# Sharing three accumulator banks between scores and projections, giving attention outputs two, and running gate tiles in halves

## The chip, the cores and the metric

The kernel runs on one core of a Trainium2 chip. The metric is the device time of one execution in microseconds (us); lower is better. PE is TensorE (matmuls), PEld its weight loads, DVE is VectorE, ACT is ScalarE, POOL is GpSimd, SP is SyncE, whose queue issues most transfers. PSUM is the memory that PE writes its sums into; this kernel uses it as eight banks of 128 x 512 fp32.

## The reference, cut to what matters

Two transformer-like blocks act on 512 tokens of width 1024. The change is in the first one:

```python
h = rmsnorm(x, norm_mix_g)
qkv_a, q_b, k_b, v_b, gate_logits = split(h @ w_in)       # 7424 columns
for gi, (window, dil) in enumerate(((128,1),(512,4),(2048,16))):
    ...   # 8 heads of 64: rmsnorm + rope on q, k; windowed attention; keep o and logsumexp
o_a = sum(softmax(lses) * outs)                          # the three groups combined
o_b = gqa_blocked_attention(q_b, k_b, v_b)               # dense, 8 query heads, 2 key heads
gates = sigmoid(gate_logits + b_gate)                    # 2 x 1024 columns
merged = gates[0] * (o_a @ w_proj_a) + gates[1] * (o_b @ w_proj_b)
x = x + merged @ w_out
...   # then top-4-of-32 experts, then the second block (two layers)
```

## The kernel before

**Order.** Python loops write out every instruction; a planner then orders them at build time, engine by engine. It walks its own estimate of the time, gives earlier-written instructions precedence among those that are ready, and hands a tile of a pool to whichever tile asks when one is free. On the chip each engine runs its list in that fixed order. `tc.issue_after(ins)` adds one rule: what is written under it comes behind `ins` on that engine.

**Precision.** Each fp32 operand is split into a high and a low part (`split`: a copy on ACT, L49, and a subtraction on DVE, L50). `mm3` (L82 to L84) makes three matmuls of each product, `mm2` (L74, L75) two.

**Stages.** `block1` runs three dilated groups (`dilated(g)`) and one `dense` stage as generators, so that the key projections of a stage are written before the last attention step of the stage ahead of it. A stage projects keys, values and queries (`proj_tok`: 24 matmuls into one PSUM tile `M`, which `headnorm` reads with two ACT copies, L277 and L278, or `split` reads for values). Then it takes four blocks of 128 tokens. In group 0 a block is four steps with two score tiles `S` each (`scores`); in groups 1 and 2 it is two steps with one score tile each (L550 to L555); in the dense stage four steps with two score tiles each. A step goes: scores on PE, row maximum on DVE (L211), exponentials on ACT (L216), transposes on PE into `T` (L231), `split` of the transposed probabilities into `Ph`, `Pl`, and `values`: matmuls into one PSUM tile `O`, which two ACT copies (L248, into `of`) or two splits (into `obh`, `obl`; some of these tiles bear the name `kzh`, `kzl`) empty.

**PSUM.** `M` has two banks, `S` two, `F` one, `T` two, `O` one: eight.

**Gate tiles.** `filler(n)` makes n of 16 gate tiles: two loads of 512 x 128 weights, each split on ACT and DVE, 24 matmuls into the `F` bank, a tanh on ACT (L363), and a store on POOL's queue. Its matmuls come behind the last matmul that was written before it. `FILL` says where: four in group 2, one behind each block (L572), and twelve in the dense stage, one in each of its first twelve steps between scores and probabilities (L506).

**Behind the attention.** `bank()` gives tiles of `S` and `M` in turn to the output projections (L605) and to `w_out` (L628, L637); `half` in `route` uses `F` and `S` for the router's logits (L703) and `O` for counts (L732). The expert stage and the second block follow.

Of the kernel before, what the change touches and what calls it, by code (L numbers as in the profile page):

```python
# [9 lines left out]
F32 = mybir.dt.float32  # L10
# [7 lines left out]
PSUM = bass.MemoryType.PSUM  # L18
# [3 lines left out]
S = 512  # L22
NT = 4
KT = 8
# [14 lines left out]
class Kern:  # L39
# [257 lines left out]

    def proj_tok(self, xh, xl, W, i, perm, ncol, ps=None):
        if ps is None:
            ps = self.psM.tile([128, 512], F32, name="M", tag="M")  # L300
        ps = ps[:, :ncol]
        sl = self.tok(i, perm)
        self.mm3(ps, [((xh[:, k, sl], xl[:, k, sl]), W[k]) for k in range(len(W))])
        return ps

    def block1(self):
        nc, tc, a = self.nc, self.tc, self.a
# [1 line left out]
        R = dict(reuse_waits="tile")  # L309
        es, pe, rs_, re = ExitStack(), ExitStack(), ExitStack(), ExitStack()  # L310
        P = lambda n, b, **k: (pe if "space" in k else es).enter_context(tc.tile_pool(name=n, bufs=b, **k))
        self.psM, self.psS, psF = (P(n, b, space=PSUM) for n, b in (("psM", 2), ("psS", 2), ("psF", 1)))
        self.psT, self.psO = P("psT", 2, space=PSUM), P("psO", 1, space=PSUM)
        self.psF = lambda: psF.tile([128, 512], F32, name="F", tag="F")
        c1 = P("c1", 1)
        O = lambda n, b: re.enter_context(tc.tile_pool(name=n, bufs=b, side="right", **R))
# [23 lines left out]
        nc.sync.dma_start(bg, a["b_gate"])  # L340
        nc.vector.tensor_scalar(bg, bg, 0.5, None, op0=ALU.mult)
        xk = [(xh[:, k], xl[:, k]) for k in range(KT)]
        todo = list(range(16))

        FILL = ((0, 0, 0, 0), (0, 0, 0, 0), (1, 1, 1, 1), (1, 1, 1, 1, 1, 1, 1, 1, 1, 1, 1, 1, 0, 0, 0, 0))
        turn = [0]

        def bank():

            turn[0] += 1  # L350
            pool, tag = (self.psS, "S") if turn[0] % 2 else (self.psM, "M")
            return pool.tile([128, 512], F32, name=tag, tag=tag)

        def filler(n=1):

            for n in [todo.pop(0) for _ in range(min(n, len(todo)))]:
                after = self.last_mm.ins
                W = self.weight(a["w_in"][:, 5376 + n * 128:5504 + n * 128], KT, 128, self.fw, 4)
                ps = self.psF()
                with tc.issue_after(after):  # L360
                    self.mm3(ps, [(W[k], xk[k]) for k in range(KT)])
                gt = stg.tile([128, S], F32, name="gl")
                nc.scalar.activation(gt, ps, AF.Tanh, scale=0.5, bias=bg[:, n:n + 1])  # L363
                self.st(GL[n], gt)
# [64 lines left out]

        def scores(q, kh, kl, mk=None):  # L430

            b = self.psS.tile([128, 512], F32, name="S", tag="S")[:, :kh.shape[-1]]
            if mk is not None:
                nc.tensor.matmul(b, lhsT=self.ident_b, rhs=mk, start=True, stop=False)
            self.mm2(b, q, kh, kl, start=mk is None)
            return b[:, None, :]
# [35 lines left out]
        def dense():  # L472
            tb = trig("b", 64)
            kA, kB = self.rope_tables(rp, *tb, a["kn_b"], 64, "kb")
            qA, qB = self.rope_tables(rp, *tb, a["qn_b"], 64, "qb")
            W = self.weight(a["w_in"][:, 5120:5376], KT, 256)
            vs = []
            for i in range(NT):
                ps = self.proj_tok(xh, xl, W, i, False, 256)
                kk = st.tile([128, 2, 2, 64], F32, name="kkb", bufs=1)  # L480
# [11 lines left out]
                if i == 1:  # L492
                    yield
            W = self.weight(a["w_in"][:, 4608:5120], KT, 512)
            q = [queries(self.proj_tok(xh, xl, W, 0, False, 512), qA, qB, 64, 0, True)]
            for i in range(NT):
# [5 lines left out]
                for p in range(4):  # L502
                    v = p // 2
                    ms = self.small.tile([128, 4], F32, name="md", bufs=4)
                    sc = [scores(q[i][:, p, s], kd[0][:, v], kd[1][:, v]) for s in range(2)]
                    filler(FILL[3][4 * i + p])  # L506
                    pr = self.probs(sc, 1, NT, SC, ms[:, :2], ms[:, 2:], True)
# [5 lines left out]
        def dilated(g, tr):  # L513
            perm = g > 0
            kA, kB = self.rope_tables(rp, *tr, a["kn_a"][g], 16, "k")
            qA, qB = self.rope_tables(rp, *tr, a["qn_a"][g], 16, "q")
            W = self.weight(a["w_in"][:, 1536 + 512 * g:2048 + 512 * g], KT, 512)
            for i in range(NT):
                ps = self.proj_tok(xh, xl, W, i, perm, 512)
                kk = st.tile([128, 8, 64], F32, name="kk", tag="qk")  # L520
                self.headnorm(ps, 8, kA, kB, 16, kk, i)
                keys(kk.rearrange("p h e -> p (h e)"), g, i)
                if i == 1:
                    yield
            W = self.weight(a["w_in"][:, 3072 + 512 * g:3584 + 512 * g], KT, 512)
            vs = []
            for i in range(NT):
                ps = self.proj_tok(xh, xl, W, i, perm, 512)
                vh = vp.tile([128, 512], F32R, name="vh")
                vl = vp.tile([128, 512], F32R, name="vl")  # L530
                self.split(vh, vl, ps)
                vs.append((vh, vl))
            W = self.weight(a["w_in"][:, 512 * g:512 + 512 * g], KT, 512)
            q = [queries(self.proj_tok(xh, xl, W, 0, perm, 512), qA, qB, 16, 0, not perm)]
            for i in range(NT):
                if i + 1 < NT:
                    q.append(queries(self.proj_tok(xh, xl, W, i + 1, perm, 512), qA, qB, 16, i + 1, not perm))
                else:
                    yield

                us = st.tile([128, 528], F32, name="us", bufs=3)
                mo_, so_ = us[:, 512:520], us[:, 520:528]
                of = st.tile([128, 4, 128], F32, name="of", bufs=1)
                sl = slice(i * 128, i * 128 + 128)
                pv = lambda j, p: tuple(t[:, p * 128:p * 128 + 128] for t in vs[j])
                if perm:
                    qh, ql = q[i]
                    mk = mask[:, 128:256] if g == 1 else m4
                    for p0 in (0, 2):
                        b = self.psS.tile([128, 2, 2, 128], F32, name="S", tag="S")  # L550
                        nc.tensor.matmul(b, lhsT=self.ident_b, rhs=mk[:, None, None, :].to_broadcast([128, 2, 2, 128]),
                                         start=True, stop=False)
                        for p in (p0, p0 + 1):
                            self.mm3(b[:, p - p0], [((qh[:, p], ql[:, p]), (kz[0][:, p, :, sl], kz[1][:, p, :, sl]))],
                                     start=False, stop=p > p0)  # L555
                        hs = slice(2 * p0, 2 * p0 + 4)
                        pr = self.probs([b.rearrange("p a s k -> p (a s) k")], 4, 1, SC, mo_[:, hs], so_[:, hs])
                        for p in (p0, p0 + 1):
                            self.values([pv(i, p)], pr[p - p0], of[:, p])
                else:  # L560
                    j0, j1 = max(0, i - 1), min(NT, i + 2)
                    mk = mask[:, (j0 - i + 1) * 128:(j1 - i + 1) * 128]
                    for p in range(4):
                        hs = slice(2 * p, 2 * p + 2)
                        ks = slice(j0 * 128, j1 * 128)
                        pr = self.probs([scores(q[i][:, p, s], kz[0][:, p, s, ks], kz[1][:, p, s, ks], mk)
                                         for s in range(2)], 1, j1 - j0, SC, mo_[:, hs], so_[:, hs])
                        self.values([pv(j, p) for j in range(j0, j1)], pr[0], of[:, p])
                ut = transposed(of.rearrange("p a t -> p (a t)"), 4)
                nc.scalar.activation(us[:, :512], ut.rearrange("p a t -> p (a t)"), AF.Copy)  # L570
                self.st(U[g][self.tok(i, perm)], us)
                filler(FILL[g][i])  # L572

        tr = {False: trig("n", 16), True: trig("p", 16)}

# [2 lines left out]
        for n in range(4):  # L578
# [2 lines left out]
                next(stages[n + 1])  # L581
            for _ in stages[n]:
                pass
        filler(16)
        rs_.close()
        at.close()
        mg = O("mg", 1)
# [10 lines left out]
        for br, w, (oh, ol) in ((0, a["w_proj_a"], oa), (1, a["w_proj_b"], ob)):  # L598
            for n in range(KT):
                if n % 4 == 0:  # L600
                    W = self.weight(w[:, n * 128:n * 128 + 512], 4, 512)
# [3 lines left out]
                ps = bank()  # L605
# [21 lines left out]
        for c, W in enumerate(Ws):  # L627
# [7 lines left out]
            for i in range(NT):  # L635
                sl, cs = slice(i * 128, i * 128 + 128), slice(c * 512, c * 512 + 512)
                ps = banks[i] if c == 0 else bank()  # L637
# [11 lines left out]
    def route(self, pool):  # L649

        nc, a, rt = self.nc, self.a, self.rt
# [39 lines left out]
        todo = []  # L691

        def half(i, c, x):
# [6 lines left out]
            xhl[i, c] = [T([128, 4, 128], f"x{s}", F32R, bufs=3) for s in "hl"]  # L700
            self.split(*xhl[i, c], p)
            self.router_act = self.last_act.ins
            ps = self.psF() if i % 2 else self.psS.tile([128, 512], F32, name="S", tag="S")  # L703
            for k in range(4):
                xh, xl = (t[:, k] for t in xhl[i, c])
                nc.tensor.matmul(ps[:, :64], lhsT=xh, rhs=Wr[:, 4 * c + k], start=k == 0, stop=False)
# [826 lines left out]
```

## Time and profile before

| what | value |
|---|---|
| median of 3 runs | 3086.06 us (3082.26 to 3087.57) |
| profiled execution | 3086.88 us, span in the trace 3085.1 us |
| PE busy | 2917.6 us (95% of the span) |
| PEld busy | 2293.6 us (74%) |
| DVE busy | 2250.2 us (73%) |
| ACT busy | 1737.4 us (56%) |
| mean granted TensorE clock | 0.982 |

Busy times are sums over one execution; the profiled execution's own time and its span differ by 1.78 us. The scores of group 0 run from 104 to 187 us, those of group 1 from 195 to 257, of group 2 from 271 to 354, of the dense stage from about 420 to 562; the output projections follow until about 650 us.

### The profile page before, as it was taken

To read this page: it belongs to the slowest core of one execution; us is meant where nothing else is said; L and a number is where in the kernel's file an instruction comes from. 1 tells how busy PE (TensorE), PEld (TensorE's weight loads), DVE (VectorE), ACT (ScalarE), POOL (GpSimd) and SP (SyncE) were. 2 spreads that over 40 slices of the span, in tenths; PEclk is the share of its full clock that TensorE was granted. 3 is DMA by queue.
4 is the path that set the end of the run, shared out by engine and by line. 5 is a ranking of instruction groups with operands and counts; after the bars stand their busy time and mean duration, and the time that the engine had idled before them with its cause. 6 is when DMAs were issued, how large, how long until landed. Compare 5 with 4: busy or idle time off the path is not lost.

```text
span 3085.1 us, 39468 instructions
## 1 busy us (share of the span) xinstructions
PE 2917.6 (95%) x14226; PEld 2293.6 (74%) x14226; DVE 2250.2 (73%) x3789; ACT 1737.4 (56%) x2577; POOL 318.4 (10%) x316
## 2 busy tenths in 40 slices
PE   7999999979999999999999997999999979999998
PEld 6898878766777666666666665878887868888876
DVE  7765577668998999999999997554466585445664
ACT  5555545337777777777777774444454234444532
POOL 0000001001112111111111101011000020110000
PEclk9999999989999999999999999999999989999999
DMA  5122233469999999999999994433536433345262
GB/s 157 63 69 67 76 107 96 129 257 318 366 365 345 354 352 360 355 359 361 356 359 359 349 368 129 133 102 114 113 103 202 148 98 115 112 118 114 89 235 89
DMA packets 405833, 644.92 MB, mean 209 GB/s; under 512 B 23024, under 2 KB 150528, under 8 KB 405632
## 3 DMA queue, kind: packets, MB, share of 16 engines
q1 hardware_dynamic: 385808, 581.67, 56.6%
q0 software_dynamic: 19248, 58.58, 6.4%
q8 instruction: 114, 1.87, 0.3%
q10 hardware_dynamic: 576, 2.10, 0.2%
q14 instruction: 87, 0.71, 0.1%
HBM read 592.10 MB, written 54.36 MB: 210 GB/s over the span
## 4 chain that ended last, share of the span: by engine, by line
PE 74%; DVE 12%; issue 7%; ACT 3%; DMA 3%; SPq 0%; POOL 0%; POOLq 0%; ACTq 0%; DVEq 0%
PE M L82 6%; PE M L83 6%; PE G L82 6%; PE M L84 6%; PE G L84 6%; PE G L83 6%; PE F L82 5%; PE F L83 5%; PE F L84 5%; DVE wlo L50 5%; PE Y L82 4%; PE Y L83 3%; PE Y L84 3%; DMA raw<-in_w_in 1%; PE O L82 1%
## 5 line engine op out<-in xcount | busy, mean ns | idle before, releaser
L50 DVE TENSOR_TENSOR wlo<-raw,whi 128x2048 fp32r<-128x2048 f32 (+4 forms) x642 | 1161.9, 1821 | 274.0 <-ACT whi L49 269.8
L49 ACT ACTIVATE whi<-raw 128x2048 fp32r<-128x2048 f32 (+3 forms) x646 | 972.1, 1532 | 231.3 <-PE M L84 110.3
L82 PE MATMUL G<-wlo,exh 128*96 128x512 f32 x1024 | 410.0, 400 | 4.7 <-ACT exh L49 2.7
L83 PE MATMUL G<-whi,exl 128*96 128x512 f32 x1024 | 404.0, 395 | 1.9 <-DVE exl L50 1.9
L84 PE MATMUL G<-whi,exh 128*96 128x512 f32 x1024 | 403.8, 394 | 0.0
L82 PE MATMUL F<-xl,whi 128*128 128x512 f32 x768 | 311.3, 405 | 17.1 <-DVE fl L1228 10.0
L83 PE MATMUL F<-xh,wlo 128*128 128x512 f32 x768 | 305.3, 398 | 2.3 <-DVE wlo L50 2.3
L84 PE MATMUL F<-xh,whi 128*128 128x512 f32 x768 | 305.6, 398 | 0.0
L82 PE MATMUL M<-wlo,xh 128*128 128x512 f32 (+2 forms) x736 | 278.1, 380 | 12.4 <-POOL wlo L50 3.5
L83 PE MATMUL M<-whi,xl 128*128 128x512 f32 (+2 forms) x736 | 275.2, 374 | 0.0
L84 PE MATMUL M<-whi,xh 128*128 128x512 f32 (+2 forms) x736 | 274.0, 374 | 0.0
L84 PEld LDWEIGHTS G<-whi,exh 128*96 128x96 f32 x1024 | 165.7, 162 | 71.5
L82 PEld LDWEIGHTS G<-wlo,exh 128*96 128x96 f32 x1024 | 165.8, 162 | 70.6 <-ACT exh L49 3.0
L82 PE MATMUL Y<-wlo,ath 128*96 128x512 f32 x512 | 207.4, 405 | 10.6 <-DVE wlo L50 9.9
L83 PEld LDWEIGHTS G<-whi,exl 128*96 128x96 f32 x1024 | 165.7, 162 | 67.3 <-DVE exl L50 2.4
L83 PE MATMUL Y<-whi,atl 128*96 128x512 f32 x512 | 202.4, 395 | 0.1
L84 PE MATMUL Y<-whi,ath 128*96 128x512 f32 x512 | 201.8, 394 | 0.0
L82 PEld LDWEIGHTS M<-wlo,xh 128*128 128x128 f32 x736 | 164.4, 223 | 32.9 <-DVE wlo L50 4.9
L82 PEld LDWEIGHTS F<-xl,whi 128*128 128x128 f32 x768 | 146.0, 190 | 54.9 <-DVE fl L1228 13.5
L83 PEld LDWEIGHTS M<-whi,xl 128*128 128x128 f32 x736 | 165.0, 224 | 13.6
L84 PEld LDWEIGHTS M<-whi,xh 128*128 128x128 f32 x736 | 164.4, 223 | 14.1
L83 PEld LDWEIGHTS F<-xh,wlo 128*128 128x128 f32 x768 | 146.2, 190 | 32.0 <-DVE wlo L50 3.0
(479 smaller groups left out, 5095.3 us busy)
## 6 DMA issues: line engine op xcount, KB each, us to landing
raw<-in_w_gate_up SPq DMA_DIRECT2D x256, 1024.0 KB, 7.0
raw<-in_w_down SPq DMA_DIRECT2D x124, 1024.0 KB, 8.2
raw<-in_w_in SPq DMA_DIRECT2D x154, 512.0 KB, 4.0
GZ<-fl POOLq DMA_DIRECT2D x80, 256.0 KB, 2.4
raw<-in_w_out SPq DMA_DIRECT2D x24, 512.0 KB, 3.9
raw<-in_w_branch SPq DMA_DIRECT2D x24, 512.0 KB, 4.4
gt<-GZ SPq DMA_DIRECT2D x48, 256.0 KB, 3.1
raw<-in_w_in SPq DMA_DIRECT2D x32, 256.0 KB, 3.1
```

The source lines that it names most:

```text
L49: self.last_act = nc.scalar.activation(hi, src, AF.Copy)
L50: self.last_dve = (eng or nc.vector).tensor_sub(lo, src, f(hi))
L82: nc.tensor.matmul(out, lhsT=ah, rhs=bl, start=start and i == 0, stop=False)
L83: nc.tensor.matmul(out, lhsT=al, rhs=bh, start=False, stop=False)
L84: self.last_mm = nc.tensor.matmul(out, lhsT=ah, rhs=bh, start=False, stop=stop and i == n - 1)
```

## The change

The pools `psM` (2) and `psS` (2) become one pool `psM` of three banks; `psO` goes from one bank to two. Gate tiles are made in halves of 12 matmuls: the first half opens the sum in `F`, the second closes it and is followed by tanh and store. The 32 halves are placed between scores and probabilities of a step: none in group 0, one in every second step of group 1 (4), one in every step of group 2 (8), and 2, 1, 1, 1 in the four steps of each dense block (20). `bank()` gives three tiles of `M` and one of `O` in turn, and the router uses `M` in place of `S`.

```diff
-        self.psM, self.psS, psF = (P(n, b, space=PSUM) for n, b in (("psM", 2), ("psS", 2), ("psF", 1)))
-        self.psT, self.psO = P("psT", 2, space=PSUM), P("psO", 1, space=PSUM)
+        self.psM, psF = (P(n, b, space=PSUM) for n, b in (("psM", 3), ("psF", 1)))
+        self.psT, self.psO = P("psT", 2, space=PSUM), P("psO", 2, space=PSUM)
...
-        todo = list(range(16))
-        FILL = ((0, 0, 0, 0), (0, 0, 0, 0), (1, 1, 1, 1), (1, 1, 1, 1, 1, 1, 1, 1, 1, 1, 1, 1, 0, 0, 0, 0))
+        todo = [(n, k0) for n in range(16) for k0 in (0, 4)]
+        FILL = ((0,) * 16, (0, 1) * 4, (1,) * 8, (2, 1, 1, 1) * 4)
...
-            pool, tag = (self.psS, "S") if turn[0] % 2 else (self.psM, "M")
+            pool, tag = (self.psM, "M") if turn[0] % 4 else (self.psO, "O")
...
-            for n in [todo.pop(0) for _ in range(min(n, len(todo)))]:
+            for n, k0 in [todo.pop(0) for _ in range(min(n, len(todo)))]:
                 after = self.last_mm.ins
-                W = self.weight(a["w_in"][:, 5376 + n * 128:5504 + n * 128], KT, 128, self.fw, 4)
-                ps = self.psF()
+                W = self.weight(a["w_in"][k0 * 128:k0 * 128 + 512, 5376 + n * 128:5504 + n * 128], 4, 128, self.fw, 4)
+                if k0 == 0:
+                    self.gbank = self.psF()
+                ps = self.gbank
                 with tc.issue_after(after):
-                    self.mm3(ps, [(W[k], xk[k]) for k in range(KT)])
+                    self.mm3(ps, [(W[k], xk[k0 + k]) for k in range(4)], start=k0 == 0, stop=k0 > 0)
+                if k0 == 0:
+                    continue
...
-            b = self.psS.tile([128, 512], F32, name="S", tag="S")[:, :kh.shape[-1]]
+            b = self.psM.tile([128, 512], F32, name="S", tag="M")[:, :kh.shape[-1]]
...
-                        b = self.psS.tile([128, 2, 2, 128], F32, name="S", tag="S")
+                        b = self.psM.tile([128, 2, 2, 128], F32, name="S", tag="M")
...
+                        filler(FILL[g][2 * i + p0 // 2])
                         hs = slice(2 * p0, 2 * p0 + 4)
...
-                filler(FILL[g][i])
...
-        filler(16)
+        filler(32)
...
-            ps = self.psF() if i % 2 else self.psS.tile([128, 512], F32, name="S", tag="S")
+            ps = self.psF() if i % 2 else self.psM.tile([128, 512], F32, name="S", tag="M")
```

## Rows read from the trace of the kernel before

**Rows 1.** The page: span, and busy time of each engine

```profile
span 3085.1 us, 39468 instructions
PE 2917.6 (95%) x14226; PEld 2293.6 (74%) x14226; DVE 2250.2 (73%) x3789; ACT 1737.4 (56%) x2577; POOL 318.4 (10%) x316
```

**Rows 2.** Busy time by stretch: length, each engine's busy us (instructions), PE clock, DMA

```profile
100.00:190.00 90.00, 80.36 (x460) 73.19 (x460) 63.23 (x190) 51.52 (x141) 9.67 (x19) 1.00 0.12 40
190.00:280.00 90.00, 82.35 (x408) 75.84 (x408) 59.70 (x153) 50.57 (x140) 1.63 (x3) 0.98 0.26 80
280.00:345.00 65.00, 63.39 (x334) 61.10 (x332) 45.95 (x129) 35.34 (x91) 1.08 (x2) 1.00 0.24 74
345.00:420.00 75.00, 67.38 (x353) 56.24 (x352) 40.61 (x135) 38.53 (x107) 4.34 (x8) 0.95 0.27 89
420.00:440.00 20.00, 16.79 (x63) 12.63 (x61) 17.18 (x47) 8.32 (x17) 3.71 (x4) 0.83 0.53 161
440.00:520.00 80.00, 78.38 (x431) 66.82 (x432) 64.56 (x164) 45.11 (x103) 10.26 (x13) 1.00 0.34 103
520.00:530.00 10.00, 9.57 (x58) 7.95 (x57) 6.46 (x19) 5.35 (x13) 0.55 (x1) 1.00 0.13 50
530.00:560.00 30.00, 21.49 (x127) 17.65 (x126) 24.64 (x72) 15.63 (x40) 5.40 (x6) 0.94 0.06 19
560.00:650.00 90.00, 88.73 (x426) 74.30 (x424) 48.94 (x80) 26.54 (x44) 3.67 (x7) 1.00 0.75 248
```

**Rows 3.** The same view in stretches of 10 us: those with a lower clock

```profile
270.00:280.00 10.00, 9.06 (x40) 7.72 (x41) 5.96 (x17) 5.19 (x21) 0.00 (x0) 0.83 0.35 118
...
370.00:380.00 10.00, 8.82 (x40) 7.79 (x39) 5.07 (x21) 4.20 (x16) 0.00 (x0) 0.66 0.08 22
...
430.00:440.00 10.00, 7.14 (x21) 5.28 (x21) 7.37 (x24) 2.67 (x6) 1.38 (x2) 0.66 0.39 112
...
550.00:560.00 10.00, 7.05 (x37) 6.00 (x38) 6.34 (x16) 3.00 (x7) 2.56 (x2) 0.83 0.00 1
```

**Rows 4.** What PE waited for between 100 and 565 us: total, times, longest

```profile
PE O L82 <- ACT of L248: 7.9, 8, 2.5
...
PE S L74 <- ACT P L216: 4.4, 7, 1.2
...
PE S L434 <- ACT P L216: 3.2, 4, 1.2
...
PE O L82 <- DVE obl L50: 1.8, 2, 1.3
...
PE S L551 <- ACT P L216: 1.6, 3, 0.7
```

**Rows 5.** Groups by line and shape, 100 to 565 us: busy, mean ns, idle before

```profile
L248 ACT ACTIVATE of<-O 64x128 f32<-64x128 f32 x96 | 26.1, 272 | 38.9 <-PE O L84 38.0
...
L50 DVE TENSOR_TENSOR wlo<-raw,whi 128x512 fp32r<-128x512 f32 x30 | 23.5, 784 | 15.4 <-ACT whi L49 15.3
...
L277 ACT ACTIVATE ht<-M 128x512 f32<-128x512 f32 x20 | 11.9, 596 | 27.2 <-PE M L84 27.1
```

**Rows 6.** The timeline: two matmuls of one gate tile, eleven matmuls apart

```profile
426.76 0.39 PE L83 MATMUL F<-xh,wlo 128*128 128x512 f32 x1
...
429.26 0.39 PE L82 MATMUL F<-xl,whi 128*128 128x512 f32 x1
```

**Rows 7.** Busy time by stretch, matmuls into `F` alone (PE, PEld, DVE, ACT)

```profile
530.00:560.00 30.00, 1.98 (x9) 1.29 (x7) 0.00 (x0) 0.69 (x1) 0.94 0.06 19
```

**Rows 8.** The same for `M`, PE alone

```profile
420.00:560.00 140.00, 0.00 (x0) 0.96 0.29 90
```

**Rows 9.** Groups by line, PE, 100 to 565 us: first matmul of each product into `M`

```profile
L82 PE MATMUL M<-wlo,xh 128*128 128x512 f32 (+1 forms) x249 | 99.8, 401 | 3.3 <-ACT kk L278 1.5 <-ACT qq L278 1.1 <-DVE vl L50 0.8
```

## Prediction

> **What bounds the kernel now.** I read the page first: PE is busy 2917.6 of 3085.1 us, so what can be won is a stretch in which PE waits [rows 1]. Then the busy times by stretch. The change acts between about 100 and 560 us; ahead of it and behind 650 us its code does nothing new. In the eight stretches shown up to 560 us PE's idle time (length minus busy) is 9.6, 7.7, 1.6, 7.6, 3.2, 1.6, 0.4 and 8.5 us, 40.3 us in all; from 560 to 650 us, the output projections, it is 1.3 us [rows 2]. So the attention stages are bound by PE with holes in it, and the projections behind them by PE alone: a us saved in the holes moves all that follows, which starts when PE gets there. The reader should also see that the holes lie at 100 to 280, 345 to 440 and 530 to 560 us, while 440 to 520 us is full.
>
> Then the clock, in stretches of 10 us. In four of them it was granted below 1: 0.83, 0.66, 0.66 and 0.83 [rows 3]. As the two levels are 1.2 and 2.4 GHz, a mean of 0.66 says that some 6.8 of the 10 us ran at the lower level and half of them, 3.4 us, were lost to a PE with work to do; the four make 1.7 + 3.4 + 3.4 + 1.7 = 10.2 us. Each follows or lies in a stretch with holes. Holes and clock together are a pool of about 50 us, 1.6% of the time: no gain can be larger.
>
> Last the waits of PE, which say what ends the holes. Outputs waiting for their one bank to be emptied: 7.9 us on ACT's copies and 1.8 us on DVE's splits. Scores waiting for exponentials to leave a score bank: 4.4 + 3.2 + 1.6 = 9.2 us [rows 4]. Projections waiting for a bank: 3.3 us [rows 9].
>
> **The change part by part.** It adds no work: the same 16 gate tiles in the same 32 weight pieces, the same matmuls, copies, loads and stores. Only banks and places change, and each price is that of a wait.
>
> *Second output bank.* The waits that it can take away are 7.9 + 1.8 = 9.7 us [rows 4]. A value tile is emptied by two copies of 0.272 us, and ACT stood idle 38.0 us before these copies, waiting for PE [rows 5]: ACT is not the one that is short. But a wait that goes exposes the next in PE's fixed order, often the transposes behind the same exponentials. Bounds 0 to 9.7; I take the middle, 5 us. The Trainium skill (Perfetto Trace Analysis, Optimizing Tensor Performance, Matmuls) asks that independent groups rotate through banks so that emptying one overlaps the next group's matmuls. The trace agrees as far as the 9.7 us of waits go, and by that rule alone the term would be 9.7.
>
> *Scores in a pool of three.* In the dense stage no projection runs between 420 and 560 us [rows 8], so the scores have three banks there for two, and the 4.4 us that its scores (L74) waited can go. In the groups projections run beside the scores, and the 3.2 us of group 0 (L434) and 1.6 us of groups 1 and 2 (L551) stay as they are. Bounds 0 to 9.2; I take 4 us, as the dense waits are short (1.2 us at most) and one more bank covers a whole score tile.
>
> *Gate tiles.* Eleven matmuls of a gate took 429.26 - 426.76 = 2.50 us, 0.227 us each [rows 6]: a half costs PE 2.7 us, a DVE subtraction of 0.784 us and an ACT copy. The dense stage goes from 12 tiles to 10: four halves, 10.9 us of PE work, leave it; group 1 gets them; group 2 keeps its four tiles, but inside its steps. From 420 to 560 us (four stretches) PE worked 126.2 us and DVE 112.8 [rows 2]. Without the four halves that is 115.3 for PE and 110 for DVE, so both are close to the limit, and the stage won't reach 115. DVE is 0.81 busy from 440 to 520 us and 0.82 from 530 to 560 us, where gates are missing (2.0 us of them [rows 7]) and PE idles 8.5 us. With gates spread over all sixteen steps I let DVE come to 0.86, so the stage takes 110 / 0.86 = 128 us for 140: 12 us less. Group 1 pays for it: 10.9 us more PE work, against 7.7 us of holes from 190 to 280 us, which are not all where the halves are; I let 4 us fall into holes and 7 us be added. Net 5 us gained. Bounds: all of the holes of 190 to 280 and 420 to 560 us, 7.7 + 3.2 + 1.6 + 0.4 + 8.5 = 21 us, and a loss of 10.9 us if the group pays in full and the dense stage stays bound by DVE at its old length.
>
> *Clock.* Of the four low stretches (10.2 us) I let one short one go, 2 us; bounds 0 to 10.2.
>
> *What the shared pool costs.* A projection holds a bank for 24 matmuls and then for two ACT copies of 0.6 us, the first 0.596 [rows 5], 1.2 us. With two banks of their own, projections ran on while one was emptied, and PE waited 3.3 us in all; there are 249 / 8 = 31 of them in the stretch [rows 9]. With two of three banks held by scores, a projection has one and pays the 1.2 us unless scores, transposes or a gate half fill it. Bounds 0 and 31 x 1.2 = 37 us; I take 3 us, the size of today's wait again, as group 2 and half of group 1 now have a gate half to fill in.
>
> *At nothing.* SP's loads of the moved gate pieces are the same 32, now earlier; they go behind projection weights in the same queue. PE had no wait on projection weights among the rows of 100 to 565 us, so they have slack; if that cover goes, a wait would show as projections waiting for `wlo`. The fixed turn of `bank()` has four tiles at once as before, and PE idles 1.3 us in its 90 us. The router's tiles get one bank more for counts and one less for logits; I cost it at nothing, at most some 1 us either way.
>
> The sum: 5 + 4 + 5 + 2 - 3 = 13 us less. From the profiled execution's 3086.9 us that is 3073.9; it stood 0.8 us above the median of the runs, so against the median 3073.
>
> **The rivals.** *Projections starve (slower).* Scores are written before most of the next stage's projections, so scores that are ready take free banks first and hold them through maximum and exponentials. Projections, which filled PE beside the attention (rows of `M` are absent only in the dense stage), then wait, and attention, which is held back by ACT and DVE, runs with less beside it. For it: the stretches 100 to 190, 190 to 280 and 345 to 420 us, where both kinds were at work with four banks between them, already hold 24.9 us of the holes [rows 2]. Against: three banks still turn over in a few us, and gate halves now stand in. It decides when the exposed drains pass the 16 us of the gains, 13 of the 31 projections; with 24 of them it costs 29 us, and the time is 3086 + 13 = 3099. The same rule of rotation in the Trainium skill speaks for this rival, since a projection left with a single bank cannot rotate; the trace of before, where projections had two, cannot show it.
>
> *Waits change names (no change).* Bank waits turn into waits on the softmax itself: outputs and scores come sooner, the transposes wait as long. Then the two bank terms are nothing, the gates' 5 us and the drains' 3 us remain: 3084. The planner may also put the halves elsewhere than their place in the text; then the gate term is missing too, and the time is the same.
>
> *The holes close (faster by more).* Halves of 2.7 us in nearly every step cover the softmax, and half of the pool of 50 us goes: 3061.
>
> **How the numbers follow.** My forecast's case (3064 to 3079) gets 0.35, holes closing 0.20, no change 0.20, starving 0.25. About 0.2%, 6 us, is what a measurement of this kernel can tell from no change. Faster is 0.35 + 0.20 = 0.55, same 0.20, slower 0.25. The likeliest gives 3073. The range goes from 3052 (two thirds of the pool, beyond which I leave 0.06) to 3095 (0.14 of the starving case lies above): 0.80 inside.
>
> **What would show each step.** Right: `O` waiting for `of` or `obl` nearly gone; L74 waiting for `P` in the dense stage gone; gate matmuls from 190 us on and in 520 to 560 us; the dense stage some 128 us long, PE's holes there below 14 us; no clock below 0.9 at its end. Wrong: matmuls into `M` or `S` waiting for L277, L278 or L216 for 10 us or more between 100 and 420 us; that stretch longer by more than 10 us; `wlo` ending PE's waits. The forecast fails most easily in the shared pool, the term with the widest bounds.

## The result, and the profile after

The changed kernel takes 3108.38 us (median of 4 runs, 3103.01 to 3110.98), the kernel before beside it 3085.99 us: a ratio of 1.0071, 95% interval 1.0055 to 1.0087. It is slower by 22 us, where the prediction said 13 us faster with a range up to 3095. The profiled execution took 3110.98 us; its span is 24.1 us longer than that of before [rows 1]. It is the longest of the four. The page first: PE is busy 12.3 us longer, with the same 14226 instructions, and idle 11.8 us longer. So half of the loss is holes, and the other half is the same work taking longer; the mean granted clock is 0.971, before 0.982.

```profile
span 3109.2 us, 39420 instructions
PE 2929.9 (94%) x14226; PEld 2306.8 (74%) x14226; DVE 2253.8 (72%) x3789; ACT 1737.3 (56%) x2577; POOL 320.1 (10%) x316
```

Three marks in the two traces say where the 24.1 us arise. The last gated sum of the first output projections (L608, after: L613) comes 6.2 us later (586.6 to 592.8 us), the router's last count (L736, L741) 15.2 us later (674.3 to 689.5), the end 24.1. So: some 6 us up to there, the attention stages above all, 9 between that mark and the router's end, 9 in the long part behind. Up to the first mark PE does 2709 matmuls in both kernels; they keep it busy 529.1 and 530.0 us, so 5.3 of the 6.2 us are holes. Behind the last mark it is idle 103.1 and 103.8 us and busy 2307.7 and 2315.9: those 9 us are nearly all the same work taking longer.

**Attention.** Busy time by stretch, after (columns as in [rows 2]):

```profile
0.00:100.00 100.00, 79.13 (x363) 65.16 (x364) 77.17 (x215) 49.63 (x89) 1.88 (x8) 0.95 0.41 127
100.00:190.00 90.00, 74.01 (x391) 65.73 (x390) 52.41 (x147) 48.43 (x124) 9.42 (x19) 0.87 0.11 33
190.00:280.00 90.00, 88.33 (x426) 83.53 (x425) 58.86 (x159) 44.14 (x114) 2.16 (x4) 1.00 0.30 92
280.00:345.00 65.00, 63.97 (x311) 61.36 (x311) 41.45 (x100) 32.90 (x72) 1.62 (x3) 1.00 0.27 82
345.00:420.00 75.00, 69.18 (x418) 61.37 (x416) 45.54 (x154) 45.99 (x147) 4.31 (x8) 0.98 0.34 107
420.00:440.00 20.00, 13.10 (x47) 9.77 (x48) 16.65 (x53) 6.51 (x15) 3.74 (x3) 0.63 0.19 54
440.00:520.00 80.00, 75.79 (x417) 63.53 (x415) 69.61 (x187) 47.81 (x106) 6.32 (x8) 1.00 0.33 100
520.00:530.00 10.00, 7.15 (x38) 5.49 (x39) 8.22 (x21) 4.62 (x12) 3.29 (x2) 1.00 0.35 117
530.00:560.00 30.00, 27.71 (x161) 23.48 (x159) 24.48 (x65) 16.38 (x40) 6.33 (x8) 1.00 0.16 51
```

Add up what PE leaves idle from 100 to 560 us: 16.0 + 1.7 + 1.0 + 5.8 + 6.9 + 4.2 + 2.9 + 2.3 = 40.8 us, against 40.3 before. The change closed holes where it was meant to (1.7 us for 7.7 from 190 to 280 us, 2.3 for 8.5 from 530 to 560), and opened as many elsewhere: 16.0 for 9.6 us in group 0, 6.9 for 3.2 at the start of the dense stage, where the clock fell to 0.87 and 0.63. And it opened one ahead of 100 us, where the prediction had looked for nothing: 79.1 us busy there, 84.0 before. What is missing shows in the matmuls into `M` alone, the projections; first before, then after:

```profile
80.00:100.00 20.00, 19.39 (x81) 16.02 (x80) 0.00 (x0) 4.43 (x8) 1.00 0.26 79
```

```profile
80.00:100.00 20.00, 4.36 (x18) 3.31 (x18) 0.00 (x0) 0.00 (x0) 0.74 0.00 1
```

Before, projections filled these 20 us, and the first product of queries and keys came at 98.7 us. After, it comes at 85.4 us, and its bank was taken long before that (the timeline of PE after: start, us, instruction; in brackets the idle time before it and its releaser):

```profile
77.65 0.39 PE L84 MATMUL M<-whi,xh 128*128 128x512 f32 x1
77.88 0.28 PE L439 MATMUL S<-mask,ident_b 128*128 128x256 bf16 x1
79.21 0.27 PE L439 MATMUL S<-mask,ident_b 128*128 128x256 bf16 x1 [1.05 <-ACT qq L278]
82.87 0.92 PE L400 MATMUL T<-ident,qq 128*128 128x128 f32 x4 [3.39 <-DVE qq L293]
85.39 0.58 PE L74 MATMUL S<-kzl,qs 128*128 128x256 f32 x1 [1.60 <-DVE qs L61]
```

A score tile of group 0 opens with a matmul that writes the mask and needs neither queries nor keys. Three of these, at 75.0, 77.9 and 79.2 us, take all three banks of the joined pool before there is a query. No bank is left for a projection, and PE idles 6.0 us until the first queries are ready. Each bank that comes free then goes to the next score tile first; the next projection starts at 95.1 us. Before, the two score banks were taken in the same way at about 4 us, but projections had two banks of their own. So PE is left with the short score tiles and the softmax between them. Its waits between 100 and 565 us (columns as in [rows 4]):

```profile
PE T L400 <- DVE qq L293: 7.9, 4, 2.3
PE T L400 <- DVE kkb L487: 4.8, 1, 4.8
PE S L439 <- ACT P L216: 3.9, 6, 1.0
PE S L74 <- DVE qs L61: 3.6, 2, 2.2
PE T L400 <- DVE kk L293: 3.6, 1, 3.6
PE S L74 <- ACT P L216: 3.2, 5, 1.0
...
PE M L82 <- ACT qq L278: 1.5, 2, 0.7
```

The outputs' waits of [rows 4] (7.9 and 1.8 us) are gone. In their place PE waits for the query and key chain on DVE (`qq`, `kkb`, `qs`, `kk`: 19.9 us, none of them among the waits before): the next tile to transpose is not normed yet, and PE's list has no projection there. That is not because none is left: two of the dense stage's query projections, 48 matmuls into `M`, run only after 450 us, where before none ran after 420 [rows 8]. Projections hardly wait for a bank to be emptied (1.5 us): in PE's fixed order the want of a bank shows as the wait of what was put ahead of the projection.

**Router.** The timeline of PE after, at the end of the router:

```profile
670.01 0.26 PE L712 MATMUL S<-r_Wr,r_xl 128*128 128x32 f32 x1
673.19 0.18 PE L740 MATMUL O<-r_selb,r_before 128*128 128x32 bf16 x1 [2.92 <-DVE r_selb L736]
673.22 0.19 PE L739 MATMUL O<-r_selb,r_ones 128*128 128x32 bf16 x1
673.66 0.80 PE L82 MATMUL O<-wlo,mh 128*128 128x512 f32 x1 [0.25 <-DVE rk L741]
674.25 0.63 PE L83 MATMUL O<-whi,ml 128*128 128x512 f32 x1
674.68 0.63 PE L84 MATMUL O<-whi,mh 128*128 128x512 f32 x1
```

`bank()` gives every fourth tile an `O` bank, so the last of 24, `w_out` for the last token tile, takes one of the two banks of the router's counts. Its matmuls start at 673.66 us, right behind a count that was read out (`rk`). They begin 0.43 us apart (674.25 to 674.68), against 0.23 us in [rows 6]: the clock is at its lower level, 1.2 GHz. Then its own token tile must still go through the router. The last addition to x, before and after (ns min/median/max, first and last start):

```profile
L640 DVE TENSOR_TENSOR x<-x,S x4: 680/688/689, 627.2 to 662.9; 128x512 f32<-128x512 f32 x4
```

```profile
L645 DVE TENSOR_TENSOR x<-x,O x2: 686/688/690, 635.4 to 681.1; 128x512 f32<-128x512 f32 x2
```

### The profile page after: what moved, and what is told of

It is laid out like the page before. It is cut to its first block, busy times and chain, and to the rows that moved or that the text cites. A ratio compares the mean times of both kernels' runs of the same rounds, so it can differ in the third digit from the quotient of the medians.

```text
span 3109.2 us, 39420 instructions
## 1 busy us (share of the span) xinstructions
PE 2929.9 (94%) x14226; PEld 2306.8 (74%) x14226; DVE 2253.8 (72%) x3789; ACT 1737.3 (56%) x2577; POOL 320.1 (10%) x316
## 5 line engine op out<-in xcount | busy, mean ns | idle before, releaser
L84 PEld LDWEIGHTS M<-whi,xh 128*128 128x128 f32 x736 | 163.6, 223 | 14.3
```

What stands on the lines that cost most here:

```text
L84: self.last_mm = nc.tensor.matmul(out, lhsT=ah, rhs=bh, start=False, stop=stop and i == n - 1)
```

## The experiments

Theory: two losses, the shared pool (projections no longer run ahead of scores) and the counts' bank; the gate halves are a gain. Main rival: the moved gates are the loss, since 420 to 440 us, which they left, is where the clock fell lowest. All ratios are to the kernel before on the same chip, with 95% intervals.

| run | median us | ratio | last gated sum | last count |
|---|---|---|---|---|
| before | 3086 | 1 | 586.6 | 674.3 |
| the change | 3108.4 | 1.0071 (1.0055 to 1.0087) | 592.8 | 689.5 |
| e1 pools alone | 3117.8 | 1.0103 (1.0088 to 1.0117) | 602.1 | 700.8 |
| e2 gates alone | 3079.1 | 0.9977 (0.9968 to 0.9985) | 577.8 | 665.5 |
| e3 counts apart | 3094.1 | 1.0027 (1.0018 to 1.0037) | 594.6 | 678.1 |
| e4 shared four | 3099.7 | 1.0041 (1.0028 to 1.0054) | 592.6 | 682.6 |
| e5 split 1 + 2 | 3113.0 | 1.0088 (1.0074 to 1.0102) | 605.9 | 692.3 |
| e6 split, halves | 3113.9 | 1.0091 (1.0076 to 1.0107) | 613.0 | 698.0 |
| e8 gates late | 3079.8 | 0.9977 (0.9968 to 0.9986) | 578.6 | 664.5 |
| e9 last tile in `O` | 3097.8 | 1.0037 (1.0024 to 1.0051) | 587.0 | 681.5 |
| e10 text order | 3128.0 | 1.0132 (1.0118 to 1.0147) | 625.4 | 713.0 |
| e11 half-bank outputs | 3087.9 | 0.9999 (0.9991 to 1.0008) | 587.3 | 673.2 |
| e12 halves, half bank | 3078.2 | 0.9972 (0.9961 to 0.9984) | 579.8 | 667.7 |
| e13 one output bank | 3103.6 | 1.0055 (1.0042 to 1.0068) | 605.5 | 687.8 |
| e14 halves in group 0 | 3097.2 | 1.0028 (1.0016 to 1.0041) | 592.8 | 677.3 |

**Pools alone, gates alone (e1, e2).** The change cut in two: e1 is the kernel before with the new pools, `bank()` and score tiles; e2 is the changed kernel with the old ones.

> The pools of the change (three banks shared by scores and projections, two for outputs, the router's tiles in them) with the whole gate tiles at their old places. Theory (the pool is the loss): all of the loss is here, a ratio of 1.006 to 1.009 (3104 to 3114 us); the first output-projection add 6 us or more later than the 567.3 us of before, projections nearly absent beside group 0's scores, and the last w_out tile behind the router's counts at about 675 us. Rival (the moved gates are the loss): 0.998 to 1.001, with the dense stage as early as before.

> The gate halves at their new places, with the pools of the kernel before. Theory (the pool is the loss): 0.997 to 1.000 (3077 to 3086 us), the dense stage ending earlier or at the same time as before, 567.3 us or less. Rival (the gates leave 400 to 440 us bare, where the clock fell): 1.002 to 1.004, holes of 7 us or more in 400 to 430 us as in the changed kernel and a first output-projection add near 574 us.

e1 loses 31.5 us, more than the whole change and more than was expected, and e2 gains 7.2: together 24 for the 22.4 measured. The pools are the loss, the halves a gain; the rival falls. With the old pools the start of the dense stage keeps its clock although the gates left it, and the holes move to where halves are now thinner (two stretches of e2):

```profile
420.00:440.00 20.00, 15.96 (x81) 12.70 (x80) 19.84 (x61) 10.43 (x22) 4.54 (x4) 1.00 0.50 146
440.00:520.00 80.00, 69.94 (x383) 58.65 (x382) 66.27 (x176) 43.08 (x103) 8.63 (x9) 0.96 0.27 83
```

**The counts' bank (e3, e9).** In the changed kernel another of each four turns takes the `O` bank; in the kernel before, the last turn is put into it.

```diff
# e3, from the changed kernel
-            pool, tag = (self.psM, "M") if turn[0] % 4 else (self.psO, "O")
+            pool, tag = (self.psM, "M") if turn[0] % 4 != 1 else (self.psO, "O")
# e9, from the kernel before
-            pool, tag = (self.psS, "S") if turn[0] % 2 else (self.psM, "M")
+            pool, tag = (self.psO, "O") if turn[0] == 24 else (self.psS, "S") if turn[0] % 2 else (self.psM, "M")
```

> The changed kernel, but of each four tiles of the output projections the first takes the output bank, not the fourth, so that the last w_out tile has a bank apart from the router's counts. Theory (the last tile waits behind the counts, and that is on the path): its last x add comes 6 to 18 us earlier than 681.1 us, the last count 6 to 9 us earlier than 689.5 us, and the ratio to before falls from 1.007 to 1.004 (3096 to 3102 us). Rival (the router's own chain or the expert gather sets the end of this stretch): the last tile is earlier, the last count is not, and the ratio stays at 1.006 to 1.008.

> The kernel before with one change: the last of the 24 turns of the output projections (w_out, last token tile, second half) takes the bank of the outputs and counts. Theory (that tile then waits for the counts of the tile before it, and all behind it comes later): its x add 10 us or more after 662.9 us, the last count 8 to 15 us after 674.3 us, ratio 1.003 to 1.005. Rival (that end is bound by the router's chain): last count within 3 us of 674.3, ratio 0.999 to 1.001.

Taking the clash out of the change gives back 14.3 us; putting it into the kernel before costs 13.1 us (13.6 and 11.4 by the ratios). At the last count it is less: e3 is there 11.4 us earlier than the change, where 6 to 9 were expected, and e9 7.2 us later than before, where 8 to 15 were expected; e3 also ended below its range. The rest lies behind, where the code is the same: there e9's PE is busy 2315.5 us, before 2307.7. The mechanism is shown from both sides, its size only to within some us; the last additions to x, e3 and then e9 (670.1 and 673.7 us, 681.1 in the change):

```profile
L645 DVE TENSOR_TENSOR x<-x,M x6: 686/687/689, 635.9 to 670.1; 128x512 f32<-128x512 f32 x6
```

```profile
L640 DVE TENSOR_TENSOR x<-x,O x1: 686/686/686, 673.7 to 673.7; 128x512 f32<-128x512 f32 x1
```

**Sharing without a lost bank (e4).** From the kernel before, no gate moved:

```diff
-        self.psM, self.psS, psF = (P(n, b, space=PSUM) for n, b in (("psM", 2), ("psS", 2), ("psF", 1)))
+        self.psM, psF = (P(n, b, space=PSUM) for n, b in (("psM", 4), ("psF", 1)))
...
-            pool, tag = (self.psS, "S") if turn[0] % 2 else (self.psM, "M")
+            pool, tag = self.psM, "M"
```

and scores and the router's logits from `psM`.

> From the kernel before: the four banks of scores and projections as one pool of four, one output bank as before, whole gate tiles at their old places. Theory (sharing lets the scores of a group run ahead of the projections that filled PE beside them): still slower, 1.001 to 1.003, with few projections beside group 0's scores. Rival (only the lost bank counts): 0.997 to 1.000, with projections beside the scores as before.

Four banks as before, only joined, cost 13.3 us, somewhat over what was expected. The first loss is where the change has it: PE busy 79.6 us of the first 100, and the projections from 80 to 100 us nearly gone (matmuls into `M`, e4):

```profile
80.00:100.00 20.00, 6.04 (x24) 4.35 (x24) 0.00 (x0) 0.23 (x1) 0.83 0.00 1
```

So joining costs without a lost bank: masks take all four here (69.6 to 79.4 us; first product at 85.6). Up to the last gated sum e4 is 6.0 us late, and most of that is PE busy longer, 534.1 us for 529.1, at a clock of 0.96 for 0.98. The rest comes behind, where the output projections and the router's logits share the pool too. The hole at the start of the dense stage is not there (PE busy 20.0 of 20 us). No run writes the mask behind the product, so how much of the loss is due to the masks is not shown.

**Banks apart, one for projections (e5, e6).** As many banks as in the change, not joined: `psM` 1, `psS` 2, `psO` 2, `bank()` taking S, O, S, M in turn so that the last tile has no `O`; e6 adds the halves.

> As many banks as in the change (three for scores and projections, two for outputs), but apart: one for projections, two for scores. Whole gate tiles at their old places; the last w_out tile not in an output bank. Theory (one ring holds projections to the order of the text, so that none passes the scores): with rings apart projections pass again, the first scores of group 0 come after 90 us and PE is busy 82 us or more of the first 100; first output-projection add no later than 571 us, ratio 0.998 to 1.002. Rival (what counts is that projections can't rotate through two banks): waits on the one bank's copies of 10 us or more, first add at 575 us or later, ratio 1.003 or more.

> The same split of banks (one for projections, two for scores, two for outputs) with the gate halves at their new places. Theory (second output bank and halves are gains, sharing alone was the loss): 0.994 to 0.998, 2 to 5 us below the halves with the old pools (3079 us). Rival (the second output bank buys nothing, or one projection bank costs more): the same as the halves with the old pools or slower, 0.998 to 1.002.

In e5 the theory failed and the rival held; e6 is slower than both of its cases. The order is that of before again (first product at 100.7 us), but a projection now waits for the bank of the one ahead of it, 34.6 us in three rows, before 5.1 (PE's waits in e5, 0 to 580 us):

```profile
PE M L82 <- DVE vl L50: 16.0, 10, 2.7
PE M L82 <- ACT qq L278: 10.5, 13, 1.2
PE M L82 <- ACT kk L278: 8.1, 9, 1.9
```

The trace agrees with the rule that the prediction cited (the Trainium skill, Perfetto Trace Analysis, Optimizing Tensor Performance, Matmuls), that independent groups should rotate through banks so that the emptying of one overlaps the next: with a single bank it does not overlap. And the halves gain nothing on top (e6): what a filler is worth depends on who holds the banks.

**Order alone (e10).** The kernel before with its own banks; projections may only not run ahead of the scores written before them.

```diff
# proj_tok; last_S is the last scores' matmul written so far
-        self.mm3(ps, [((xh[:, k, sl], xl[:, k, sl]), W[k]) for k in range(len(W))])
+        with self.tc.issue_after(self.last_S.ins) if self.last_S else ExitStack():
+            self.mm3(ps, [((xh[:, k, sl], xl[:, k, sl]), W[k]) for k in range(len(W))])
```

> The kernel before with its own banks untouched; each projection of the attention stages is only ordered on PE behind the scores that stand ahead of it in the text, which is the order that a ring shared by both imposes. Theory (the loss of the shared pool is this order): the first scores of group 0 before 80 us, few projections in 80 to 100 us, PE busy 79 to 80 us of the first 100, the first output-projection add 5 to 12 us after 567.3 us, ratio 1.002 to 1.005. Rival (the loss is in the banks themselves, in who holds them and how long): ratio 0.999 to 1.001 and the first add within 3 us of 567.3.

The direction is right, the size is not: 41 us lost, where 6 to 15 were expected, and the first product at 89.5 us, not before 80. (In the change it comes at 85.4; what starts at 75 us there are masks.) The projections of 80 to 100 us go as they did in the change:

```profile
80.00:100.00 20.00, 2.13 (x10) 1.43 (x8) 0.00 (x0) 2.17 (x4) 0.67 0.00 0
```

So losing the projections' lead is enough to lose more than the shared pool does; but this edit is stricter than the pool, and does not show that order is all of the pool's cost, nor, as the expectation put it, that a shared pool hands its banks out strictly in the order of the text.

**The second output bank (e11, e12, e13).** e11 and e12 let outputs alternate between two halves of the old bank; e13 is e3 with `psO` 1, the eighth bank left empty.

```diff
# e11 from the kernel before, e12 from e2; obank is one tile of two halves
-        o = self.psO.tile([128, 2, 128], F32, name="O", tag="O")
+        self.oturn = 1 - self.oturn
+        o = self.obank[:, self.oturn]
```

> The kernel before with its pools; the attention outputs alternate between the two halves of their one bank, so that outputs have a second buffer and nobody loses a bank. Old gate tiles and places. If the second output buffer is worth its forecast: PE's waits of outputs on the copies and splits gone, 3 to 9 us less, ratio 0.997 to 0.999. Rival (the waits change names, or a half can't be written while the other is emptied): 0.999 to 1.001.

> Old pools, gate halves at their new places, and outputs in alternating halves of their bank: the parts of the change that are gains by themselves, without the shared pool. If they add up: 0.994 to 0.997 (3066 to 3076 us), faster than the halves alone (3079 us). Rival (one wait hides behind the other): 0.997 to 0.999.

> The changed kernel with the counts apart (3094.1 us, ratio 1.0027), less the second output bank, which is left empty: the difference is what that bank is worth. If it is worth the forecast 5 us or more: waits of outputs on their copies come back with some 8 us, the first output-projection add 4 to 9 us later, ratio 1.004 to 1.006. Rival (waits change names): the waits come back, but the ratio stays within 1.002 to 1.0035.

e11 does not answer the question: the wait that it should have removed is still there (8 times, as before), so no second buffer came of it (PE's waits, 100 to 565 us).

```profile
PE O L82 <- ACT of L249: 7.8, 8, 2.5
```

e12 has the same outputs, so it doesn't answer either; it equals e2 within their intervals. e13 does answer: without the second bank the change, counts apart, is 9.5 us slower (8.6 by the ratios). Not by the row that the forecast was read from, though. Outputs wait for their copies only 1.3 us in e13, where some 8 were expected (same window as above); what grew is the transposes' wait for `Pl` (2.9 us in e3), and PE's busy time from 440 to 520 us is 74.0 us, 76.6 in e3. How the missing bank brings that about is not shown; e13 also leaves the output projections and the counts one bank fewer.

```profile
PE T L231 <- DVE Pl L50: 8.8, 4, 2.7
...
PE O L82 <- ACT of L248: 1.3, 4, 0.5
```

**Where the halves go (e8, e14).** e8 is e2 with group 1's four halves moved to the dense stage; e14 is e3 with eight halves of the dense stage in group 0's steps.

```diff
-        FILL = ((0,) * 16, (0, 1) * 4, (1,) * 8, (2, 1, 1, 1) * 4)
+        FILL = ((0,) * 16, (0,) * 8, (1,) * 8, (2, 1, 2, 1) * 4)        # e8
+        FILL = ((0, 1) * 8, (0, 1) * 4, (1,) * 8, (1, 1, 1, 0) * 4)     # e14
```

> The old pools and the halves, but none in group 1 and 24 instead of 20 in the dense stage. If group 1's halves fill holes there: slower than with them by 2 to 5 us, 0.998 to 1.001. If the dense stage, where PE was busy 69.9 of 80 us from 440 to 520 us with 20 halves, has room for the four more: as fast or faster, 0.995 to 0.998.

> The changed kernel with the counts apart, and eight of the dense stage's halves moved into the steps of group 0, where the projections no longer run beside the scores. Theory (group 0 loses because PE has nothing beside the softmax, and other work can stand in): PE busy 78 us or more from 100 to 190 us (73.9 without), its clock there 0.95 or more (0.87 without), ratio 1.001 or less. Rival (the eight halves only move holes: the dense stage misses them): ratio 1.002 to 1.004.

e8 is e2 again: the halves' placement in group 1 is worth nothing that shows. In e14 the halves fill group 0 (78.9 us busy for 73.9, clock 0.96 for 0.87) and are missed in the dense stage (71.0 for 76.6): the rival held, and the time stays (1.0028 for e3's 1.0027).

```profile
100.00:190.00 90.00, 78.93 (x440) 68.75 (x438) 53.02 (x146) 48.91 (x124) 11.59 (x23) 0.96 0.19 60
...
440.00:520.00 80.00, 70.99 (x374) 59.66 (x374) 70.26 (x193) 44.24 (x98) 8.36 (x8) 0.94 0.29 87
```

## Why the prediction was wrong

It failed at two steps: *what the shared pool costs*, 3 us, and the router's tiles, *at nothing*.

- **At nothing: "I cost it at nothing, at most some 1 us either way."** Measured 11 to 14 us (e9 and e3, by ratios and by medians), half of the loss or more. The step counted banks (four at once, as before) and did not follow whose bank it was: the last tile of a fixed turn fell into the bank of the counts, which depend on the tiles ahead of it. The wait was readable before: 24 turns, the last one a multiple of four, and L732 taking `O`.
- **What the shared pool costs: 3 us, bounds 0 and 37.** An estimate from the runs: e1's 31.5 us, less 14 for the counts, plus the 9 that the second output bank gives back, is some 27 us; the joining alone, with no bank lost, is 13.3 us (e4), though that has the router's logits in the joined pool too. The bounds held it, the choice between them didn't. And the reasoning, a drain of 1.2 us exposed per projection, was not what happened: projections wait 1.5 us for their banks in the change. Nor did a projection always have "one" bank, as the step took for granted. The drains are what a single bank of its own costs (e5: 34.6 us of waits). In the joined pool score tiles take the banks ahead of projections, in group 0 before there is a query (all three from 79.2 to 85.4 us), and PE runs dry where the softmax and the query chain are the only work in its list: from 78 to 190 us and at the start of the dense stage.
- **The starving rival** named the place and the cause (scores first, attention with less beside it) and had 0.25. But it had scores that are ready take the banks, and the trace shows that scores that are not ready take them too. It priced it by drains, at 13 us over before, and left out the counts. The sign that it set, 10 us of waits of `M` or `S` for L277, L278 or L216 from 100 to 420 us, did not come: in the larger stretch of 100 to 565 us these rows make 1.5 + 3.9 + 3.2 = 8.6 us. The starved PE showed as waits for the chain that it ran up against (19.9 us), not for banks.
- **Second output bank: 5 us, bounds 0 to 9.7.** The sign was right and the size at the upper bound, 9 us in the shared pool (e13); alone, in the old pools, it wasn't separated. That the price came near is luck: it was read from the outputs' waits, and in the joined pools these are nearly gone without the second bank too (1.3 us).
- **Scores in a pool of three: 4 us.** Hardly seen. Scores' waits for exponentials in the dense stage went from 4.4 to 3.2 us, in group 0 from 3.2 to 3.9, and only the 1.6 us of groups 1 and 2 are gone; the sign named for it, the dense wait gone, did not come.
- **Gate tiles: 5 us gained.** Right in sign and near in size: 7 us alone (e2, 0.9977, interval 0.9968 to 0.9985), 9.5 in the shared pool (e1 against the change). Where it comes from was only partly as argued: group 1's share made no difference (e8), and the gain is not all holes. Up to the last gated sum e2 is 8.8 us ahead; 7.1 of them are PE's busy time for the same 2709 matmuls, at a clock of 0.99 for 0.98. In e8 it is 3.0 of 8.0, so the division is not a steady one.
- **Clock: 2 us gained.** The other way: 190 to 280 us came from 0.98 to 1.00 and 530 to 560 us from 0.94 to 1.00 [rows 2], but 100 to 190 us went from 1.00 to 0.87 and 420 to 440 us from 0.83 to 0.63. Up to the last gated sum it is 0.95 for 0.98, but PE's busy time there grew by only 0.9 us, no more than it varies (e9 and e11, the same up to there but for e11's outputs, have 530.2 and 530.3 for 529.1). In the change what counts there is the holes, 5.3 us; in the whole trace busy time makes 12.3 of the 24.1 us.

With the sizes of the runs, the sum would have been -9 for the output bank, -7 for the gates, +27 for the pool, +14 for the counts: 25 us slower, against 22.4. That it fits is no test: the 27 was made from e1, the 14 and the 9, so all that is left of the sum is e1 and e2.

Open: from the last count to the end of the trace the kernels of this study take between 2409.0 and 2419.7 us, before 2410.8, the change 2419.7. The code of that part is unaltered. As said above, the change's excess there is PE busy longer, not PE idle longer. Executions of the kernel before differ among themselves in the same way: of 67 with the clock on record, 13 had a mean granted clock of 0.982 and took 3083.6 us on average, 9 had 0.978 and took 3090.7; the change's four had 0.971 to 0.974. So several of its last 9 us may be no more than the spread of one execution. Not explained either is why order alone (e10) costs three times the joined pool.

No version was found to beat the halves in the old pools: e2, e8 and e12, 3078 to 3080 us, are one result, 0.2 to 0.3% below the kernel before.

## What to carry to other kernels

Before joining two pools, ask what each pool of its own allowed: here two banks that only projections could take kept work running ahead of a latency-bound softmax, and that lead was worth more than the waits that the shared banks removed. Ask too what the first instruction of a tile needs: one that opens with a mask is ready at any time, and it holds its bank from then on (here 8 to 10 us) before it can use it. Follow each tile of a fixed turn to its last one and ask who else lives in that bank; a tile that ends up behind something that depends on its neighbours costs the whole chain behind it, however few banks are short. And count the holes over the whole stage, the part ahead of the edit too: a gain that only moves holes shows as an unchanged sum (40.3 and 40.8 us).

## What the runs showed of the hardware

- The granted clock fell where PE had little to do, and stayed low into full work. In the change, by 10 us:

```profile
400.00:410.00 10.00, 8.54 (x43) 6.88 (x42) 5.89 (x19) 2.80 (x7) 0.00 (x0) 1.00 0.44 149
410.00:420.00 10.00, 5.87 (x34) 4.79 (x32) 6.05 (x36) 4.67 (x14) 0.54 (x1) 0.88 0.07 29
420.00:430.00 10.00, 3.10 (x9) 1.64 (x9) 9.34 (x35) 2.87 (x6) 1.37 (x1) 0.50 0.11 27
430.00:440.00 10.00, 10.00 (x39) 8.13 (x40) 7.31 (x19) 3.63 (x9) 2.37 (x3) 0.76 0.28 80
```

PE is 5.9 and 3.1 us busy from 410 to 430 us, the clock is at its lower level (0.50) for the whole of the second of these, and it is still below 1 in the next 10 us, in which PE has no idle time at all.
- Filling such a hole brings the clock back (e14: 0.87 to 0.96 in group 0 with eight halves more), and opening another one loses it again (1.00 to 0.94 from 440 to 520 us), so that the time did not change.
